# A fifth projection joins the four that are accumulated part by part in the first stage

## The chip, the core and the metric

The kernel runs on one NeuronCore of a Trainium2 chip. Its metric is the device time of one launch in microseconds (us), less being better. Five engines take part: TensorE (PE in the profile, its weight loads PEld), VectorE (DVE), ScalarE (ACT), GpSimd (POOL) and SyncE (SP), which issues nearly all DMA transfers here. Each engine runs its own instructions in a fixed order and waits where an operand or a buffer is not ready.

## The reference

A decoder block on 512 tokens of width 1024. The part that matters here is its beginning:

```python
ada = silu(c) @ w_ada + b_ada                 # 6 vectors of 1024
h = x * (1 + scale1) + shift1
proj = h @ w_in                               # 512 x 2304
qa, ka, va, qb, kb, vb = split(proj)
oa = sliding_window_attention(qa, ka, va)     # 8 heads, 2 key/value heads
ob = stick_breaking_attention(qb, kb, vb)     # 8 heads
mix = concat(rms_norm(oa), rms_norm(ob)) @ w_out
x = layer_norm(alpha * x + gate1 * mix)
```

After it come a second modulation and the PEER layer (product-key retrieval over 16384 experts, computed densely for three of the four token blocks and by gathered rows for the fourth), then the second layer norm.

## The kernel before, in words

All fp32 matrix products are made of three passes. A tile is split into a high part (ACT, a copy to the matmul's type, line 93) and a low part (DVE, the difference, line 94), and high times high, high times low and low times high are accumulated in PSUM. In the profile's names, `hhi` and `hlo` are the two halves of the modulated input, `uhi`/`ulo` and `wpre` those of a projection's weights, `vwhi`/`vwlo` those of the value projection.

**First stage.** The modulation needs `scale1` and `shift1`, and these need 2 x 4 MB of adaLN weights. The work is cut into four parts of 256 columns (PARTS). For each part SP issues the adaLN weights (`wah`, line 212) and the input's columns (`oT`, line 246); PE multiplies the weights by silu(c) (line 221, tile `adap`), ACT copies the result (`rows`, line 224), PE sums it over partitions into four columns (line 227, tile `zada`), DVE adds the bias and makes `sc` (lines 230, 232), and ACT and DVE modulate and split the part's two chunks (lines 266, 268, 93, 94). Four projections are accumulated along with the parts (`half_proj`, line 275): six products of 128 x 512 for each part and projection. They are q and k of the first two pairs of stick-breaking heads. Their weights are loaded by `load_head` (line 251) with parts 0 and 1. What a projection lacks when the last part is modulated is added by `proj_chunk`, which also copies the result out of PSUM (ACT, line 306).

`zada` is a tile of three PSUM banks. The column sums use the first bank, a few warm-up products the second, and the third is free. The same three banks are the score tile `z` of the stick-breaking attention (`sb_weights`): its first product (line 368) waits until `zada` is done with.

**What follows.** In the order of the program text: weights of the first stick-breaking pair (`sb`, high priority), q and k of the second pair, the value projection of the second half of the columns (`proj_v(1)`, line 323, 96 products of 320 columns), `qa` of the first pair of local heads (`proj_chunk(9)`, line 304, 24 products), the gate of the second sub-layer (`ada_rows(5)`: eight multiply-adds on DVE, lines 171 and 173, on weights `wa` loaded at line 167, and a column sum on PE, line 190), the value projection of the first half (`proj_v(0)`), the values of the first pair (`sbv`), the second pair, the other gate (`ada_rows(2)`) and so on. The loads of `wa` and the three tiles of a value projection (`vwraw`, `vwhi`, `vwlo`) share four buffers (tag `big`), so a load waits there until a DVE or PE instruction has freed one.

The order on each engine is set by the Tile framework's scheduler, from the program text and priorities. It mixes these pieces, so that on PE the products of one stand between those of another.

Of the kernel before, what the change touches and what calls it, by code (L numbers as in the profile page):

```python
# [8 lines left out]
F32 = mybir.dt.float32  # L9
F32R = mybir.dt.float32r  # L10
# [10 lines left out]
P = 128  # L21
D = 1024
DC = 8
S = 512
# [21 lines left out]
PARTS = ((0, 2), (2, 4), (4, 6), (6, 8))  # L46
# [8 lines left out]
GROUP = 6  # L55
OWN = 14
PRE = 0

CW = 80
STAIR = [(0, 1, 16, 0), (1, 1, 8, 16), (2, 1, 5, 24), (3, 1, 4, 32),  # L60
# [8 lines left out]
def tile_block(ctx, tc, xr, xT, ccol, wada, bcol, brow, wqk, wv, sinks, gncol, wout,  # L69
               ln1c, ln1r, wq, keys, u_rows, uT, v_rows, ln2r, out):  # L70
    nc = tc.nc
# [20 lines left out]
    def split(src, hi, lo, eng=None):  # L92
        A.activation(hi, src, AF.Copy)  # L93
        (eng or V).tensor_tensor(lo, src, hi.bitcast(F32), op=OP.subtract)  # L94

    def load_split(src, shape, tag, pool, eng=None, rawtag=None, rawbufs=None):
        raw = pool.tile(shape, F32, name=f"{tag}raw", tag=rawtag or f"{tag}raw", bufs=rawbufs)
        nc.sync.dma_start(raw, src)
        hi = pool.tile(shape, F32R, name=f"{tag}hi", tag=f"{tag}hi")
        lo = pool.tile(shape, F32R, name=f"{tag}lo", tag=f"{tag}lo")  # L100
        split(raw, hi, lo, eng)
        return hi, lo
# [40 lines left out]
    with ExitStack() as front:  # L143
# [4 lines left out]
        fw = fw_cm.__enter__()  # L148
        ps = front.enter_context(tc.tile_pool(name="psf", bufs=2, space=PSUM))
# [43 lines left out]
        def load_w_in(i):  # L193
            return load_split(wqk[i].rearrange("p (c n) -> p c n", c=DC), [P, DC, P], "u", wsp)
# [10 lines left out]
        def ada_load(h):  # L205
            c0, c1 = PARTS[h]
            wpart[h] = []
            for q in range(2):
                w = fa.tile([P, 2560], F32, name="wah", tag="big", bufs=BIG)[:, :2048].rearrange(
                    "p (c g n) -> p c g n", c=4, g=2)  # L210
                for g in range(2):
                    nc.sync.dma_start(w[:, :, g], wada[g].rearrange("p (c n) -> p c n", c=DC)[
                        :, 4 * q:4 * q + 4, c0 * P:c1 * P])
                wpart[h].append(w)

        def ada_part(h):
            c0, c1 = PARTS[h]
            p = ps.tile([P, 512], F32, name="adap", tag="o", bufs=1)
            for q, w in enumerate(wpart.pop(h)):
                for j in range(4):  # L220
                    T.matmul(p[32 * j:32 * j + 32, :], srep[:, 4 * q + j], w[:, j].rearrange("p g n -> p (g n)"),
                             start=(q == 0), stop=(q == 1), skip_group_check=True)
            rows = fa.tile([P, D], F32, name="rows", tag="acc")[:, :512]
            A.activation(rows, p, AF.Copy)
            cols = zada[:, 4 * h:4 * h + 4]
            for n in range(4):
                T.matmul(cols[:, n:n + 1], rows[:, n * P:(n + 1) * P], part, start=True, stop=True,
                         skip_group_check=True)
            for g in range(2):
                V.tensor_tensor(adac[:, g * 8 + c0:g * 8 + c1], cols[:, 2 * g:2 * g + 2], bc[:, g * 8 + c0:g * 8 + c1],  # L230
                                op=OP.add)
            V.tensor_scalar(sc1[:, c0:c1], adac[:, 8 + c0:8 + c1], 1.0, None, op0=OP.add)
# [3 lines left out]
        heads = []  # L236
        zada = ps.tile([P, 1536], F32, name="zada", tag="z", bufs=1)

        def warm(n):
            for _ in range(n):  # L240
                T.matmul(zada[:, 512:512 + P], ones, ones, start=True, stop=True, skip_group_check=True)


        def load_x(h):
            for dc in range(*PARTS[h]):
                nc.sync.dma_start(oT[:, dc], xT[:, dc * S:(dc + 1) * S])

        def load_head(i):
            raw = wsp.tile([P, DC, P], F32, name="uraw", tag="uraw") if i < 2 else fw.tile(
                [P, 1536], F32, name="hraw", tag="e", bufs=2)[:, :D].rearrange("p (c n) -> p c n", c=DC)  # L250
            nc.sync.dma_start(raw, wqk[i].rearrange("p (c n) -> p c n", c=DC))
            if i < 2:
                t = [wsp.tile([P, DC, P], F32R, name=f"u{e}", tag=f"u{e}") for e in ("hi", "lo")]
            elif i == 2:
                t = [fw.tile([P, DC, P], F32R, name=f"wpre{e}", tag="prs", bufs=3) for e in range(2)]
            else:
                both = fw.tile([P, 2560], F32R, name="wpre", tag="vr", bufs=1)
                t = [both[:, k * D:(k + 1) * D].rearrange("p (c n) -> p c n", c=DC) for k in range(2)]
            split(raw, *t)
            heads.append((t, ps.tile([P, S], F32, name="pj", tag="mmss"[i], bufs=2)))  # L260

        def modulate(h):
            for dc in range(*PARTS[h]):
                xt = oT[:, dc]
                if dc % 2:
                    A.activation(xt, xt, AF.Identity, scale=sc1[:, dc:dc + 1], bias=adac[:, dc:dc + 1])
                else:
                    V.tensor_scalar(xt, xt, sc1[:, dc:dc + 1], adac[:, dc:dc + 1], op0=OP.mult, op1=OP.add)
                split(xt, hhi[:, dc], hlo[:, dc])

        def half_proj(i, h):
            (hi, lo), p = heads[i]
            for dc in range(*PARTS[h]):
                for n, (a, b) in enumerate(((hi, hhi), (hi, hlo), (lo, hhi))):
                    T.matmul(p, a[:, dc], b[:, dc], start=(dc == 0 and n == 0), stop=(dc == DC - 1 and n == 2))

        warm(WARM[0])
        for h in range(len(PARTS)):
            ada_load(h)
            load_x(h)  # L280
            if h < 2:
                load_head(2 * h)
                load_head(2 * h + 1)
            with tc.high_priority():
                ada_part(h)
                if h == 0:
                    warm(WARM[1])
                modulate(h)
            if h == len(PARTS) - 1:
                break  # L290
            for i in range(min(4, 2 * h + 2)):
                for g in range(h + 1) if i >= 2 * h else (h,):
                    half_proj(i, g)

        def proj_chunk(i, nm):
            if i < 4:
                half_proj(i, len(PARTS) - 1)
                p = heads[i][1]
            else:
                hi, lo = load_w_in(i)  # L300
                p = ps.tile([P, S], F32, name="pj", tag="m", bufs=2)
                for dc in range(DC):
                    for n, (a, b) in enumerate(((hi, hhi), (hi, hlo), (lo, hhi))):
                        T.matmul(p, a[:, dc], b[:, dc], start=(dc == 0 and n == 0), stop=(dc == DC - 1 and n == 2))  # L304
            o = fw.tile([P, S], F32, name=nm, tag=nm)
            A.activation(o, p, AF.Copy, scale=0.125 if nm[0] == "q" else 1.0)
            return o
# [155 lines left out]
        def sb(j, q, k):  # L463
            with tc.high_priority():
                return sb_weights(q, k)

        def sbv(j, w):
            with tc.high_priority():
                sb_values(j, w)

        w = sb(0, proj_chunk(0, "q"), proj_chunk(1, "k"))
        q0, k0 = proj_chunk(2, "q"), proj_chunk(3, "k")
        proj_v(1)
        qa = proj_chunk(9, "qa")
        ada_rows(5, gate2, 1)
        proj_v(0)
        sbv(0, w)
        w = sb(1, q0, k0)
        ada_rows(2, gate1, 0)
        q0, k0 = proj_chunk(4, "q"), proj_chunk(5, "k")  # L480
        sbv(1, w)
        ka = proj_chunk(8, "ka")
        w = sb(2, q0, k0)
# [3 lines left out]
        q0, k0 = proj_chunk(6, "q"), proj_chunk(7, "k")  # L487
# [3 lines left out]
        w = sb(3, q0, k0)  # L491
# [27 lines left out]
        p = ps.tile([P, S], F32, name="ssp", tag="o", bufs=1)  # L519
# [30 lines left out]
        for tb in (1, 2, 3, 0):  # L550
            t = slice(tb * P, (tb + 1) * P)
            zg = [[ps.tile([P, 512], F32, name="zm", tag="ms"[g]) for _ in range(2)] for g in range(2)]
            for n_c, c in enumerate(ORDER):
                hi, lo = wo[c]
# [40 lines left out]
    ps = ctx.enter_context(tc.tile_pool(name="psm", bufs=1, space=PSUM, reuse_waits="tile"))  # L595
# [47 lines left out]
    for hp in range(NHP):  # L643
        hi, lo = load_split(wq[hp].rearrange("p (c n) -> p c n", c=DC), [P, DC, P], "u", wsp, G)
        p = bank("h", "pq", bufs=2)
# [187 lines left out]
    for i in range(groups):  # L833
# [5 lines left out]
        p = banks[i] = bank(f"y{2 + i % 4}", "pw")  # L839
# [156 lines left out]
    plan = [[] for _ in range(NK + 1)]  # L996
    todo = list(range(PRE, 2 * P))
    for n, t in enumerate(todo):
# [52 lines left out]

    for n in range(min(RING, PRE)):
        fetch(n)
    while len(stash) < LOOK:
        u_slot(len(stash), bank("h", "ph", bufs=2), ring.tile([P, ND], F32, name="stash"), V if len(stash) < LOOK - LG else G)
    for n in range(PRE):
        unit(n)
        if n + RING < PRE:
            fetch(n + RING)
# [20 lines left out]
    for i in range(NK):  # L1080
# [6 lines left out]
        p = u_mm(i + LOOK) if i + LOOK < NK else None  # L1087
# [103 lines left out]
```

## Time and profile before

| | us |
|---|---|
| median of 3 runs | 1593.63 |
| lowest and highest | 1587.36, 1598.72 |
| the profiled execution's own time | 1593.33 |
| its span | 1591.6 |
| PE busy | 1552.4 (98%) |
| DVE busy | 1220.5 (77%) |
| ACT busy | 647.0 (41%) |
| POOL busy | 457.4 (29%) |

The profile is of one execution. Its own time differs from the span by 1.7 us of start and end, and from the median by 0.3 us. The attention part that the change touches takes the first 300 us; the PEER layer takes the rest. A matmul's end is modelled and matmuls overlap, so that the distance between starts says how fast they pass, and the duration of one row does not.

### The profile page before, as it was taken

How to read it: one execution, taken by the hardware profiler on the slowest of the kernel's cores; microseconds unless marked ns; L12 is line 12 of the kernel's file. 1: busy time of each engine (PE TensorE's matmuls, PEld its weight loads, DVE VectorE, ACT ScalarE, POOL GpSimd, SP SyncE). 2: the span in 40 equal slices, each digit the busy share in tenths (PEclk: the TensorE clock that was granted, in tenths of full speed). 3: DMA queues.
4: the chain of work that ended last, by engine and by line, in shares of the span. 5: the costliest groups of instructions: out<-in, count | busy, mean ns of one | idle time of the engine just before them, and what ended most of it. 6: DMA issues, size and time to landing. Idle time of an engine off the chain costs nothing.

```text
span 1591.6 us, 21979 instructions
## 1 busy us (share of the span) xinstructions
PE 1552.4 (98%) x8109; PEld 1344.7 (84%) x8109; DVE 1220.5 (77%) x2351; ACT 647.0 (41%) x935; POOL 457.4 (29%) x410
## 2 busy tenths in 40 slices
PE   8999999999989999999999999999999999999997
PEld 5776766788879999899999999999999999998885
DVE  3568485599999997578777777777777777777887
ACT  2535574433354554333333333333333333333340
POOL 0002133544400000334333333333433344333100
PEclk9999899999999999999999999999999999999998
DMA  9563132222225655999999989999898998989872
GB/s 339 198 257 146 53 125 87 92 81 80 93 89 190 225 212 212 328 333 321 310 305 314 316 294 312 310 309 322 295 309 308 314 315 300 313 281 313 269 248 83
DMA packets 147356, 382.12 MB, mean 240 GB/s; under 512 B 11312, under 2 KB 68656, under 8 KB 143280
## 3 DMA queue, kind: packets, MB, share of 16 engines
q1 hardware_dynamic: 110384, 246.49, 44.6%
q0 software_dynamic: 36864, 134.23, 24.6%
q8 instruction: 63, 1.03, 0.3%
q14 instruction: 45, 0.37, 0.1%
HBM read 351.32 MB, written 29.36 MB: 239 GB/s over the span
## 4 chain that ended last, share of the span: by engine, by line
PE 77%; DVE 13%; DMA 4%; ACT 3%; issue 1%; SPq 1%; POOL 1%; DVEq 0%; ACTq 0%; POOLq 0%
PE yb L991 32%; PE ph L981 25%; PE pw L842 5%; PE ph L807 4%; PE pj L304 3%; PE zm L557 2%; DVE scr L621 1%; DMA wa<-in_wada_dram 1%; DVE tsi L623 1%; DVE tsi L620 1%; DMA wah<-in_wada_dram 1%; PE pq L648 1%; DVE tsv L622 1%; DVE tsv L619 1%; PE z L368 1%
## 5 line engine op out<-in xcount | busy, mean ns | idle before, releaser
L856 POOL DMA_INDIRECT gat<-in_u_rows_dram,idx x128 | 162.5, 1269 | 477.6 <-DVE hd L874 226.7
L94 DVE TENSOR_TENSOR ulo<-uraw,uhi 128x1024 fp32r<-128x1024 f32 x133 | 162.7, 1225 | 164.8 <-ACT uhi L93 160.4
L981 PE MATMUL ph<-h2hi,ulo 128*128 128x384 f32 x768 | 258.6, 337 | 0.6 <-DVE ulo L94 0.6
L981 PE MATMUL ph<-h2hi,uhi 128*128 128x384 f32 x768 | 258.2, 336 | 0.6 <-ACT uhi L93 0.6
L981 PE MATMUL ph<-h2lo,uhi 128*128 128x384 f32 x768 | 258.1, 336 | 0.0
L856 POOL DMA_INDIRECT gat<-in_v_rows_dram,idx x128 | 162.1, 1267 | 263.6 <-DVE y L884 227.0
L991 PE MATMUL yb<-vhi,ghi 128*128 128x512 f32 x630 | 195.6, 391 | 0.0
L991 PE MATMUL yb<-vhi,glo 128*128 128x512 f32 x630 | 195.5, 391 | 0.0
L991 PE MATMUL yb<-vlo,ghi 128*128 128x512 f32 x630 | 195.2, 391 | 0.0
L93 ACT ACTIVATE uhi<-uraw 128x1024 fp32r<-128x1024 f32 x155 | 162.3, 1049 | 74.8 <-PE pq L648 52.9
L884 DVE SCALAR_TENSOR_TENSOR y<-gat,cf,y 128x1024 f32<-128x1024 f32 x127 | 162.9, 1283 | 2.8 <-DMA gat<-in_v_rows_dram,idx 0.5
L874 DVE CUSTOM_DVE_ANT_0 gscr<-gat,h2row 128x1024 f32<-128x1024 f32 x128 | 156.5, 1223 | 9.6 <-DMA gat<-in_u_rows_dram,idx 7.2
L1098 ACT ACTIVATE stash<-ph 128x384 f32<-128x384 f32 x96 | 47.2, 492 | 274.9 <-PE ph L981 274.9
L981 PEld LDWEIGHTS ph<-h2hi,uhi 128*128 128x128 f32 x768 | 144.4, 188 | 4.7 <-ACT uhi L93 1.0
L981 PEld LDWEIGHTS ph<-h2lo,uhi 128*128 128x128 f32 x768 | 144.4, 188 | 4.4
L981 PEld LDWEIGHTS ph<-h2hi,ulo 128*128 128x128 f32 x768 | 144.3, 188 | 1.0 <-DVE ulo L94 1.0
L991 PEld LDWEIGHTS yb<-vlo,ghi 128*128 128x128 f32 x630 | 118.2, 188 | 26.3
L991 PEld LDWEIGHTS yb<-vhi,glo 128*128 128x128 f32 x630 | 118.3, 188 | 25.8
L94 DVE TENSOR_TENSOR vlo<-vraw,vhi 128x1024 fp32r<-128x1024 f32 x97 | 118.5, 1222 | 18.9 <-ACT vhi L93 18.3
L991 PEld LDWEIGHTS yb<-vhi,ghi 128*128 128x128 f32 x630 | 117.3, 188 | 17.9
L93 ACT ACTIVATE vhi<-vraw 128x1024 fp32r<-128x1024 f32 x97 | 102.8, 1060 | 56.4 <-issue 39.5
L958 ACT ACTIVATE ghi<-gt 128x384 fp32r<-128x384 f32 x97 | 51.0, 526 | 175.4 <-DVE gt L924 175.4
(311 smaller groups left out, 2898.2 us busy)
## 6 DMA issues: line engine op xcount, KB each, us to landing
uraw<-in_uT_dram SPq DMA_DIRECT2D x128, 512.0 KB
vraw<-in_v_rows_dram SPq DMA_DIRECT2D x128, 512.0 KB
w_d<-stage SPq DMA_DIRECT2D x12, 2048.0 KB
wt<-w_d SPq DMA_DIRECT2D x32, 768.0 KB
wa<-in_wada_dram SPq DMA_DIRECT2D x16, 1024.0 KB
wah<-in_wada_dram SPq DMA_DIRECT2D x16, 512.0 KB
uraw<-in_wq_dram SPq DMA_DIRECT2D x16, 512.0 KB
uraw<-in_wqk_dram SPq DMA_DIRECT2D x11, 512.0 KB
```

Source lines behind the costliest of these rows:

```text
L93: A.activation(hi, src, AF.Copy)
L94: (eng or V).tensor_tensor(lo, src, hi.bitcast(F32), op=OP.subtract)
L304: T.matmul(p, a[:, dc], b[:, dc], start=(dc == 0 and n == 0), stop=(dc == DC - 1 and n == 2))
L807: T.matmul(p[:, :ND], a[:, dc], b[:, dc, P:], start=(dc == 0 and n == 0), stop=(dc == DC - 1 and n == 2))
L842: T.matmul(p[:, k * P:(k + 1) * P], oh4[:, 1, :, k], oh4[:, 2 + j, :, k], start=(j == 0), stop=(j == 1), skip_group_check=True)
L856: G.indirect_dma_start(out=t, out_offset=None, in_=rows, in_offset=bass.IndirectOffsetOnAxis(ap=idx[:, k:k + 1], axis=0))
L874: V.tensor_tensor_reduce(out=scr, in0=t, in1=h2row, scale=1.0, scalar=0.0, op0=OP.mult, op1=OP.add, accum_out=hd[:, n:n + 1])
L884: V.scalar_tensor_tensor(y0, t, cf[:, k:k + 1], y0, op0=OP.mult, op1=OP.add)
L958: A.activation(gop[i][0], gts[i], AF.Copy)
L981: T.matmul(p[:, :ND], a[:, dc], b[:, dc, P:], start=(dc == 0 and n == 0), stop=(dc == DC - 1 and n == 2))
L991: T.matmul(ybank[b][c0 // 512][:, c0 % 512:(c1 - 1) % 512 + 1], x[:, t], y[:, c0:c1], start=(i == 0 and n == 0), stop=(n == 2 and i == (NK ...
L1098: A.activation(stash[i + LOOK], p[:, :ND], AF.Gelu_apprx_tanh)
```

## The change

The table FRONT names the projections of the first stage, now five: 0 to 3 and 9, the queries `qa` of the first pair of local heads. The fifth's weights are loaded and split with part 2, into buffers of tiles that the attention uses later (the raw weights in one of the two `e` buffers, where the raw weights of heads 2 and 3 were, the halves in `sphi` and `splo`). Its result goes into the third bank of `zada`. The products of its first three parts are written behind those of the four, and `proj_chunk(9)` is called ahead of `sb(0, ...)` and no longer behind `proj_v(1)`. Line numbers of the changed kernel are higher by 1 to 8 than those before.

```diff
+FRONT = (0, 1, 2, 3, 9)
...
-            nc.sync.dma_start(raw, wqk[i].rearrange("p (c n) -> p c n", c=DC))
+            nc.sync.dma_start(raw, wqk[FRONT[i]].rearrange("p (c n) -> p c n", c=DC))
...
+            elif i == 4:
+                t = [fw.tile([P, 1536], F32R, name=f"wpre{e}", tag=f"sp{e}", bufs=1)[:, :D].rearrange(
+                    "p (c n) -> p c n", c=DC) for e in ("hi", "lo")]
...
-            heads.append((t, ps.tile([P, S], F32, name="pj", tag="mmss"[i], bufs=2)))
+            heads.append((t, zada[:, 1024:] if i == 4 else ps.tile([P, S], F32, name="pj", tag="mmss"[i], bufs=2)))
...
                 load_head(2 * h + 1)
+            elif h == 2:
+                load_head(4)
             with tc.high_priority():
                 ada_part(h)
...
-            for i in range(min(4, 2 * h + 2)):
+            for i in range(min(len(FRONT), 2 * h + 2)):
                 for g in range(h + 1) if i >= 2 * h else (h,):
                     half_proj(i, g)
 
         def proj_chunk(i, nm):
-            if i < 4:
-                half_proj(i, len(PARTS) - 1)
-                p = heads[i][1]
+            if i in FRONT:
+                n = FRONT.index(i)
+                half_proj(n, len(PARTS) - 1)
+                p = heads[n][1]
...
-        w = sb(0, proj_chunk(0, "q"), proj_chunk(1, "k"))
+        q0, k0 = proj_chunk(0, "q"), proj_chunk(1, "k")
+        qa = proj_chunk(FRONT[4], "qa")
+        w = sb(0, q0, k0)
         q0, k0 = proj_chunk(2, "q"), proj_chunk(3, "k")
         proj_v(1)
-        qa = proj_chunk(9, "qa")
         ada_rows(5, gate2, 1)
```

PE, first stage, from the last part's second adaLN product to the first products on its modulated input. Before (`wpre_200`, `wpre_201` are the halves of the third projection's weights, `wpre` those of the fourth, `part` the constant of the column sum):

```order
L221 MATMUL adap<-wah,srep 32x512 x4
L275 MATMUL pj<-hlo,wpre_200 128x512
L275 MATMUL pj<-hhi,wpre_201 128x512
L275 MATMUL pj<-hhi,wpre_200 128x512
...
L227 MATMUL zada<-part,rows 128x1 x4
L275 MATMUL pj<-hhi,wpre_201 128x512
L275 MATMUL pj<-hlo,wpre 128x512
L275 MATMUL pj<-hhi,wpre 128x512 x2
...
L275 MATMUL pj<-hhi,uhi 128x512 x2
```

And now:

```order
L222 MATMUL adap<-wah,srep 32x512 x4
L279 MATMUL pj<-hhi,wpre 128x512
L279 MATMUL pj<-hlo,wpre 128x512
L279 MATMUL pj<-hhi,wpre 128x512
L279 MATMUL zada<-hhi,wprehi 128x512
L279 MATMUL zada<-hlo,wprehi 128x512
L279 MATMUL zada<-hhi,wprelo 128x512
...
L228 MATMUL zada<-part,rows 128x1 x4
L279 MATMUL pj<-hhi,uhi 128x512 x2
L279 MATMUL zada<-hhi,wprehi 128x512
```

Before, four products stand between the adaLN product and the column sum, and six behind it. Now the six stand ahead of it, 18 products of the fifth projection too, and none between it and the products that need the modulated input.

ACT, from the split of the last part's input (`hhi`) to the first score tile (`e<-z`). Before:

```order
L93 ACTIVATE hhi<-oT 128x512 x2
L306 ACTIVATE q<-pj 128x512
L93 ACTIVATE vwhi<-vwraw 128x2560
L306 ACTIVATE k<-pj 128x512
L306 ACTIVATE q<-pj 128x512
...
L93 ACTIVATE uhi<-uraw 128x1024 x2
L371 ACTIVATE e<-z 128x1280
L372 ACTIVATE e<-e 128x1280
```

And now:

```order
L94 ACTIVATE hhi<-oT 128x512 x2
L94 ACTIVATE vwhi<-vwraw 128x2560
L313 ACTIVATE q<-pj 128x512
L94 ACTIVATE uhi<-uraw 128x1024
L313 ACTIVATE k<-pj 128x512
L313 ACTIVATE qa<-zada 128x512
L94 ACTIVATE uhi<-uraw 128x1024
L378 ACTIVATE e<-z 128x1280
L313 ACTIVATE q<-pj 128x512
L379 ACTIVATE e<-e 128x1280
L313 ACTIVATE k<-pj 128x512
L380 ACTIVATE e<-e 128x1280
```

The split of the value weights now stands ahead of the first q, the copy of `qa` ahead of the scores, and the copies of the second pair's q and k between the steps on the score tile.

PE, from the end of the value projection of the second half to that of the first (both on `vwhi`, `vwlo`). Before:

```order
L323 MATMUL pj<-vwhi,hlo 128x320
L304 MATMUL pj<-hhi,uhi 128x512
L304 MATMUL pj<-hlo,uhi 128x512
L304 MATMUL pj<-hhi,ulo 128x512
...
L383 MATMUL z<-sphi,negtri 128x512 x2
...
L383 MATMUL z<-splo,negtri 128x512 x2
...
L190 MATMUL adap<-acc,ones 128x512 x2
L368 MATMUL z<-q,k 128x512
...
L323 MATMUL pj<-vwhi,hhi 128x320
```

And now:

```order
L330 MATMUL pj<-vwhi,hlo 128x320
L191 MATMUL adap<-acc,ones 128x512 x2
L330 MATMUL pj<-vwhi,hhi 128x320 x2
L390 MATMUL z<-sphi,negtri 128x512 x2
...
L330 MATMUL pj<-vwlo,hhi 128x320
```

The 24 products on `uhi`, `ulo` are gone from here. Two products of the next value projection stand ahead of the `sphi` products; the `splo` products and the next pair's `z<-q,k` now stand inside that projection.

## Rows read from the trace of the kernel before

**Rows 1.** Busy time by engine, the page: time, share of the span, instructions.
```profile
PE 1552.4 (98%) x8109; PEld 1344.7 (84%) x8109; DVE 1220.5 (77%) x2351; ACT 647.0 (41%) x935; POOL 457.4 (29%) x410
```

**Rows 2.** Stretches: engines' busy us (instructions), then PE clock, DMA share, GB/s.
```profile
0.00:40.00 40.00, 32.89 (x168) 22.69 (x168) 12.39 (x31) 11.79 (x17) 2.57 (x11) 0.91 1.00 339
40.00:56.00 16.00, 15.23 (x74) 10.28 (x75) 4.38 (x9) 7.01 (x11) 0.00 (x0) 1.00 0.41 156
```

**Rows 3.** PE in time, last part: start, us, instruction [idle before, releaser].
```profile
41.51 1.06 PE L221 MATMUL adap<-wah,srep 128*32 128x512 f32 x8
...
47.06 0.95 PE L227 MATMUL zada<-part,rows 128*128 128x1 f32 x8
...
49.90 0.73 PE L275 MATMUL pj<-hhi,uhi 128*128 128x512 f32 x2 [0.40 <-ACT hhi L93]
...
55.83 2.42 PE L368 MATMUL z<-q,k 64*128 64x512 f32 x8
```

**Rows 4.** PE in time, 77 to 90 us.
```profile
77.40 0.40 PE L304 MATMUL pj<-hhi,uhi 128*128 128x512 f32 x1
...
82.29 0.40 PE L304 MATMUL pj<-hhi,uhi 128*128 128x512 f32 x1
...
84.39 0.85 PE L383 MATMUL z<-splo,negtri 128*128 128x512 f32 x3
...
85.54 1.93 PE L190 MATMUL adap<-acc,ones 128*128 128x512 f32 x4
87.40 2.42 PE L368 MATMUL z<-q,k 64*128 64x512 f32 x8
89.75 0.42 PE L323 MATMUL pj<-vwhi,hhi 128*128 128x320 f32 x1
```

**Rows 5.** PE in time, the end of the first value sums.
```profile
107.74 0.44 PE L399 MATMUL oacc<-e,vr 128*64 128x128 f32 x4 [0.53 <-ACT vr L325]
108.47 1.98 PE L190 MATMUL adap<-acc,ones 128*128 128x512 f32 x4 [0.29 <-DVE acc L173]
```

**Rows 6.** ACT in time.
```profile
49.23 1.14 ACT L93 ACTIVATE hhi<-oT 128x512 fp32r<-128x512 f32 x2
...
52.79 2.34 ACT L93 ACTIVATE vwhi<-vwraw 128x2560 fp32r<-128x2560 f32 x1
...
56.45 2.02 ACT L93 ACTIVATE uhi<-uraw 128x1024 fp32r<-128x1024 f32 x2
58.34 1.26 ACT L371 ACTIVATE e<-z 128x1280 f32<-128x1280 f32 x1
...
81.05 1.49 ACT L93 ACTIVATE sphi<-e 128x1536 fp32r<-128x1536 f32 x1 [2.40 <-DVE e L378]
```

**Rows 7.** DVE in time.
```profile
27.21 2.36 DVE L94 TENSOR_TENSOR wpre<-hraw,wpre 128x1024 fp32r<-128x1024 f32 x2 [0.18 <-ACT wpre L93]
...
55.16 2.83 DVE L94 TENSOR_TENSOR vwlo<-vwraw,vwhi 128x2560 fp32r<-128x2560 f32 x1 [3.99 <-ACT vwhi L93]
...
62.24 1.49 DVE L375 SCALAR_TENSOR_TENSOR e<-z,e 128x1280 f32<-128x1280 f32 x1
...
65.80 1.28 DVE L173 SCALAR_TENSOR_TENSOR acc<-wa,silu,acc 128x1024 f32<-128x1024 f32 x1
...
84.83 2.82 DVE L94 TENSOR_TENSOR vwlo<-vwraw,vwhi 128x2560 fp32r<-128x2560 f32 x1 [0.50 <-ACT vwhi L93]
```

**Rows 8.** The chain that ended last: start, us, what; an issue to its landing.
```profile
67.11 6.89 DMA wa<-in_wada_dram
...
76.73 5.70 DMA vwraw<-in_wv_dram
```

**Rows 9.** SP's DMA issues in time, adaLN weights of the last part.
```profile
25.75 5.01 SPq L212 DMA_DIRECT2D wah<-in_wada_dram  x4
```

**Rows 10.** Stretches at the lower clock, columns as in rows 2.
```profile
26.20:30.00 3.80, 3.80 (x10) 2.80 (x9) 3.20 (x4) 1.92 (x3) 0.00 (x0) 0.55 1.09 356
183.80:197.40 13.60, 13.60 (x52) 10.15 (x50) 3.56 (x5) 4.05 (x6) 0.99 (x1) 0.51 0.20 68
```

## The prediction, made before the changed kernel ran

> **What bounds the kernel now.** The busy table first: PE is busy 98% of the span [rows 1], so nearly every microsecond taken off PE, or filled where it waits, counts in full. The change touches the first 115 us alone; behind that the order of the engines is the old one but for small swaps inside the attention. So I read PE in order of time there, asking where it waits. While the adaLN weights come in (0 to 40 us) PE is busy 32.9 of 40 us with 339 GB/s moving; from 40 to 56 us it is busy 15.2 of 16 [rows 2]. In the second stretch the fifth projection's products land. There PE waits 0.40 us in one place, for the split of the last part's input [rows 3]. Then PE runs on, and the qa products that are to move stand between 77.40 and 84.4 us [rows 4].
>
> **Their price where they are.** From the first to the 22nd qa product the starts lie 82.29 - 77.40 = 4.89 us apart over 21 steps, 0.233 us each [rows 4]; 24 cost 5.6 us. They cost the same in the first stage. Moving them gains only the PE idle time that they fill, less any that they open. What did they cover? ACT splits the value weights of proj_v(0) when the load issued at 76.73 us has landed 5.70 us later [rows 8], DVE takes the low part until 84.83 + 2.82 = 87.65 us [rows 7], and PE starts on them at 89.75 us [rows 4]. The qa products are that wait's cover, and it goes.
>
> **Part by part.**
>
> *The load.* 512 KB more on SP ahead of the last part's adaLN weights. Its raw buffer is free when DVE has split the third projection's weights, the first of two at 27.21 us, so at 27.21 + 1.18 = 28.4 [rows 7]; SP would have gone on at 25.75 [rows 9] and now does about 0.5 us after 28.4, some 3.1 us later. Queued behind it are those weights, the last input chunks and the value weights. Bytes up to the last adaLN weights: 16 x 0.524 MB of them, 1.57 MB of input, 4 + 1 heads of 0.524 MB, 12.6 MB; at 339 GB/s [rows 2] 37.1 us. PE comes to them at 41.51 us or later [rows 3]. Cost 0, with 4 us of cover; if it were gone, up to 3.1 us.
>
> *The split.* One more split of 128 x 1024 on ACT and DVE, about 1.0 and 1.2 us (half of the pairs in [rows 6] and [rows 7]), behind the third part's modulation, where DVE is busy 4.4 of 16 us [rows 2]. Cost 0; the same split goes further on.
>
> *The last part.* The column sum started at 47.06 us, and the first product on the modulated input at 49.90 [rows 3]. Of these 2.84 us the sums take 0.81 (the chain through DVE and ACT the rest), and six leftover products fill 1.4. In the new order the six and 18 of the fifth stand ahead of the sums and none behind. So the sums start 24 x 0.233 = 5.6 us later, at 52.7, the first product at 55.5, and PE stands 2.0 us in place of about 0.5: **+1.5 us**.
>
> *The scores.* The first score product waits for the copies of k and now of qa, since qa lies in its tile. ACT ends the split of the input at 50.37 + 5.6 = 56.0, then 2.34 for the value weights, and q, a weight split, k and qa at 0.5, 1.0, 0.5, 0.5 (a copy of 128 x 512 takes half of the `hhi` pair's 1.14, a split half of 2.02 [rows 6], less a little overlap): 60.9. PE has 23 products first, 0.237 apart as in the last part now (25 starts from 49.90 to 55.83 [rows 3]): 55.5 + 5.4 = 60.9. A tie; the scores start at 61.0 in place of 55.83 [rows 3], cost 0.1. The attention's chain is thus 5.2 us later, and 6.1 from DVE's step at 62.24 us [rows 7] on, as two copies of 0.5 now stand between ACT's steps.
>
> *The value weights of proj_v(0).* Their load waits for the last multiply-add of ada_rows(5); that for a load issued when the fourth (65.80 us [rows 7]) frees its buffer. In the new order the fourth stands right behind DVE's attention step, which ends at 63.73 + 6.1 = 69.8; it ends at 71.1, 4.0 us later. With 6.89 and 5.70 us from issue to landing as now [rows 8], the low part is ready at 87.65 + 4.0 = 91.6. PE: scores until 63.4, seven products (1.6), proj_v(1) with what is mixed in as before (from 58.2 to 77.40, 19.2 and one product), the gate's sums 1.86 (85.54 to 87.40): ready at 86.3. The high part comes at 88.8, then `sphi` 1.49 behind it on ACT [rows 6] at 90.3. PE waits 2.5 + 1.2 + 0.2: **+3.9**. The old waits of 0.53 and 0.29 us further on [rows 5] should go, as PE is later than what they wait for: **-0.8**.
>
> *Sum:* 1.5 + 0.1 + 3.9 - 0.8 = +4.7 us. By the other route: behind 91.6 PE has what it had from 89.75 to 110.45 us (108.47 + 1.98 [rows 5]) less 0.8 of waits, with 3.5 of `splo` and `z<-q,k` products that stood ahead (1.15 and 2.35 [rows 4]): 91.6 + 23.1 = 114.7 against 110.45, +4.3. I take +4. Bounds of the largest term: if only the value split's delay (58.4 against 55.13, 3.2) reaches it, +3.5 in the sum; if the load keeps its time, the wait is 1.3 and the sum +2; if all 6.1 reach it, +6.5.
>
> **The clock, left out of the sum.** TensorE fell to the lower level, 1.2 GHz, at 26.2 us, after sums over partitions and an idle stretch, for 3.8 us (granted 0.55), and at 183.8 for 13.6 us (0.51), behind column sums of ada_cols [rows 10]. The first costs 3.8 x 0.45 = 1.7 us, the second 13.6 x 0.49 = 6.7. The two new waits resemble the first, 0 to 1.7 each. The new order puts full products between the two column sums at 180 to 190 us: 0 to -6.7. Nothing of before decides these, so 0 in the sum and both ends in the range.
>
> **A rule that speaks against this.** In 40 to 56 us weight loads are busy 10.28 of 16 us [rows 2], yet 25 products start one behind the other from 49.90 to 55.83 us, 0.237 apart [rows 3]. The Trainium skill (Perfetto Trace Analysis, Identifying the Most-Contended Engine) calls matmul busy time a poor measure and has headroom judged by LDWEIGHTS busy share and FLOPs. By it this stretch has 5.7 us to spare and the fifth projection would fit free; the trace's start distances do not agree.
>
> **Rivals.**
> 1. *The room is there* and the products pass in the first stage beside the others. For it: weight loads 64% busy. Against: start distances. Even so the low part of proj_v(0)'s weights comes at 87.65 as now, PE has 23.1 us behind it, and 110.75 stands against 110.45: **1593.6 us**, no change. To gain the 5.6 us, that load would have to move too.
> 2. *Faster:* the low-clock stretch at 183.8 goes. Mechanism: the 14 `sphi` and `splo` products that now stand between the two column sums keep the clock up. Against: ahead of 183.8 small value products and score products on 64 rows had run as well, and these remain. It decides if over 4 of the 6.7 us are saved: 1593.3 + 4.3 - 6.7 = **1591 us**.
> 3. *Clearly slower:* both new waits drop the clock (3.4) and the value weights come at the upper bound (6.5): **1603 us**. It would need two stretches as long as that at 183.8 (13.4) to pass 1609.
> 4. *The load starves the last part* (SP held at 28.4): up to 3.1 more, **1600 us**. Against: 4 us of cover.
>
> **How the numbers follow.** The profiled execution took 1593.33 us, 0.3 under the median, so the sum may be laid on either: 1593.3 + 4 = **1597 us**. Chances: forecast (1595 to 1600) 0.55; rival 1, 0.14; rival 2, 0.16; rivals 3 and 4 up to 1609, 0.12; beyond, 0.03. The range leaves out the outer tails: runs of before lie 6 us below and 5 above their median, so 1589 to 1604. About 1% (16 us) is what a measurement of this kernel can tell from no change: all cases but the last lie within it, so faster 0.02, same 0.94, slower 0.04.
>
> **What would show it.** Right: PE idle about 2 us ahead of the last part's first product (some 55.5 us); scores at 61; proj_v(0)'s low part ready at about 91.6 with PE waiting 3 to 4 us ahead of it; the next projection on `uhi` at 114 to 115 in place of 110.45. Wrong: if the scores start at 56 to 58 (rival 1), if the clock stays up through 180 to 200 (rival 2), if the last part's adaLN product waits for a DMA (rival 4), or if the attention behind 115 us gives the 4 us back from waits that I took to shift with it.

## The result, and the profile after

The changed kernel takes **1601.28 us** (median of 14 runs, 1598.34 to 1606.18) against 1593.55 of the kernel before on the same chip; the ratio is 1.0059, 95% interval 1.0046 to 1.0073. That is 7 to 12 us slower and inside the 1% that I called no change. The forecast was 1597, range 1589 to 1604. The profiled execution took 1603.71 us, its span 1602.0. It lies 2.4 us above the median of its runs, so the two profiles are 10.4 us apart where the medians are 7.7.

The stretches of the changed kernel show where its engines differ (columns as in [rows 2]: busy us of PE, its weight loads, DVE, ACT and POOL, then PE clock, DMA share, GB/s):

```profile
40.00:56.00 16.00, 13.62 (x68) 9.35 (x69) 3.84 (x8) 4.26 (x7) 0.00 (x0) 1.00 0.51 195
77.00:90.00 13.00, 10.80 (x57) 8.31 (x55) 6.52 (x8) 7.29 (x7) 2.45 (x4) 1.00 0.40 142
90.00:115.00 25.00, 23.39 (x128) 19.28 (x129) 14.28 (x10) 4.65 (x6) 2.24 (x2) 0.93 0.66 231
184.00:198.00 14.00, 14.00 (x89) 10.89 (x88) 7.21 (x8) 5.43 (x8) 0.77 (x2) 0.87 0.35 114
258.00:276.00 18.00, 11.91 (x31) 7.96 (x29) 12.26 (x23) 7.45 (x11) 4.72 (x2) 0.72 0.66 234
```

Two of these stretches in the kernel before:

```profile
90.00:115.00 25.00, 24.15 (x136) 19.14 (x136) 14.01 (x13) 6.38 (x9) 0.51 (x1) 1.00 0.82 307
258.00:276.00 18.00, 17.00 (x76) 13.57 (x75) 13.34 (x26) 6.89 (x12) 10.01 (x4) 0.98 0.45 154
```

Three things stand there. PE stands longer than before at 40 to 56 and 77 to 115 us, as forecast. At 184 to 198 us its clock is 0.87, where [rows 10] show 0.51; the low stretch is not gone, it comes some 10 us later and lasts about half as long, with 0.81, 0.50 and 0.84 in the three stretches of 4 us from 192 to 204:

```profile
196.00:200.00 4.00, 4.00 (x18) 3.07 (x17) 0.00 (x0) 1.18 (x3) 0.00 (x0) 0.50 0.20 78
```

And at 258 to 276 us, far behind the change, PE is busy 11.91 us in place of 17.00, at a clock of 0.72. The last I had not looked at: it is the largest.

The starts of the same work in the profiled executions tell where each microsecond came and went. The three right columns are experiments, below.

| start of, us | before | changed | after_oldmap | before_newmap | after_lng_behind |
|---|---|---|---|---|---|
| first product of the last part | 49.90 | 55.64 | 55.45 | 51.75 | 55.87 |
| projection behind proj_v(0) | 110.38 | 117.28 | 115.48 | 111.99 | 116.22 |
| values of the third pair | 197.62 | 201.48 | 196.42 | 199.39 | 197.15 |
| column sums `ssp` | 251.2 | 255.6 | 250.6 | 253.2 | 251.4 |
| first transposes `zt` | 264.6 | 276.4 | 264.2 | 273.0 | 265.6 |
| first `pq` | 310.7 | 324.0 | 310.2 | 319.1 | 313.7 |
| last `yb<-vhi,ghi` | 1513.9 | 1528.2 | 1513.3 | 1522.7 | 1516.5 |
| span | 1591.6 | 1602.0 | 1588.4 | 1597.9 | 1592.1 |

Read the column of the changed kernel against before: +5.7, +6.9, then +3.9 and +4.4 (some 3 us come back), then +11.8 and +13.3 within 60 us, and +14.3 to the end of the long stage. The last stretch, 73.8 us in place of 77.7, gives 3.9 back.

**The first part.** PE of the changed kernel in time, around the last part (answers to [rows 3]):

```profile
52.80 0.95 PE L228 MATMUL zada<-part,rows 128*128 128x1 f32 x8
55.64 0.73 PE L279 MATMUL pj<-hhi,uhi 128*128 128x512 f32 x2 [1.89 <-ACT hhi L94]
...
61.19 1.98 PE L375 MATMUL z<-q,k 64*128 64x512 f32 x5
```

The sums start at 52.80 (forecast 52.7), the first product at 55.64 (55.5) after 1.89 us of waiting (2.0), the scores at 61.19 (61.0). Then PE around proj_v(0) of the changed kernel:

```profile
90.77 0.56 PE L330 MATMUL pj<-vwhi,hhi 128*128 128x320 f32 x2 [2.97 <-ACT vwhi L94]
92.15 1.43 PE L390 MATMUL z<-sphi,negtri 128*128 128x512 f32 x3 [0.81 <-ACT sphi L94]
```

and DVE, whose multiply-adds free the buffer for that load and which makes the low part:

```profile
73.58 1.28 DVE L174 SCALAR_TENSOR_TENSOR acc<-wa,silu,acc 128x1024 f32<-128x1024 f32 x1 [1.73 <-DMA wa<-in_wada_dram]
...
90.75 2.82 DVE L95 TENSOR_TENSOR vwlo<-vwraw,vwhi 128x2560 fp32r<-128x2560 f32 x1 [1.62 <-ACT vwhi L94]
```

The load was issued at 80.40 us and landed 8.0 us later, not 5.70 as in [rows 8], so the low part is ready at 93.57 (forecast 91.6). PE waits 2.97 + 0.81 us and 1.06 for `splo` at 76.6. The `negtri` products at 92.15 also run at the lower clock (0.57 granted from 92 to 96 us): three in 1.43 us, where three took 0.85 at 84.39 us before [rows 4].

**The second loss.** SP issues its transfers in order. Its DMA issues behind the attention, changed kernel:

```profile
257.63 0.33 SPq L545 DMA_DIRECT2D lng<-in_ln1r_dram  x1
258.06 0.38 SPq L547 DMA_DIRECT2D lnb<-in_ln1r_dram  x1
258.49 0.42 SPq L549 DMA_DIRECT2D l1c<-in_ln1c_dram  x1
258.96 1.50 SPq L568 DMA_DIRECT2D r<-in_xr_dram  x3
```

and before:

```profile
229.65 0.33 SPq L537 DMA_DIRECT2D lng<-in_ln1r_dram  x1
231.44 0.33 SPq L539 DMA_DIRECT2D lnb<-in_ln1r_dram  x1
231.82 0.42 SPq L541 DMA_DIRECT2D l1c<-in_ln1c_dram  x1
232.30 2.40 SPq L560 DMA_DIRECT2D r<-in_xr_dram  x3
```

The same transfers stand some 27 us later. SP's longest wait between 225 and 262 us in the changed kernel (what waited for what, us in total, times, longest):

```profile
SPq L545 <- PE ssp L530: 23.8, 1, 23.8
```

The layer norm's scale `lng` now waits for the column sums `ssp`, which have nothing to do with it. Behind it on SP wait `r`, the block's input rows. The chain of waits of the changed kernel goes through just that (start, us, what):

```profile
258.96 6.37 DMA r<-in_xr_dram
265.33 0.02 issue
265.35 1.06 ACT r L569
266.42 0.03 issue
266.44 0.81 DVE r L573 x2
```

In the kernel before, that DVE step starts at 257.77. The reason is not in any order of instructions. The change gives the tags `sphi` and `splo` their first tiles in the fifth load, earlier than before, and the pool lays tags out in order of first use. Addresses of the two built programs, in bytes of a partition:

```
                        lies over, before      lies over, changed
lng  113888 to 117984   k, sphi                neg, sqa
lnb  117984 to 122080   sphi, splo             sqa, sink, dist, q
sqa's own place         102016 to 106112       114304 to 118400
```

`sqa` is what the `ssp` sums read, so it is free only when they end.

### The profile page after: what moved, and what is told of

It is laid out like the page before. It is cut to its first block, busy times and chain, and to the rows that moved or that the text cites. A ratio compares the mean times of both kernels' runs of the same rounds, so it can differ in the third digit from the quotient of the medians.

```text
span 1602.0 us, 21970 instructions
## 1 busy us (share of the span) xinstructions
PE 1553.3 (97%) x8109; PEld 1345.2 (84%) x8109; DVE 1224.7 (76%) x2351; ACT 647.9 (40%) x935; POOL 457.1 (29%) x410
## 4 chain that ended last, share of the span: by engine, by line
PE 81%; DVE 11%; DMA 3%; ACT 2%; issue 1%; POOL 0%; SPq 0%; DVEq 0%; ACTq 0%; POOLq 0%
PE yb L999 33%; PE ph L989 25%; PE pw L850 5%; PE ph L815 4%; PE pj L311 3%; PE zm L565 2%; DVE scr L629 1%; PE pj L279 1%; DVE tsi L631 1%; DVE tsi L628 1%; PE pj L330 1%; PE z L375 1%; PE pq L656 1%; DVE tsv L630 1%; DVE ulo L95 1%
```

## The experiments

All ratios are to the kernel before on the same chip, with 95% intervals; times are medians. The runs were taken on several chips, so that ratios, not times, are compared between them. In the cuts of code, `...` stands for lines left out.

### The memory map, both ways

**before_newmap**: the kernel before with only the tiles' first use moved.

```
+            elif h == 2:
+                for e in ("hi", "lo"):
+                    fw.tile([P, 1536], F32R, name=f"held{e}", tag=f"sp{e}", bufs=1)
```

> The kernel before with one thing of the change alone: the memory map. Two tiles with the tags sphi and splo are allocated (and never used) where the change first allocates them, so that the tiles allocated later move up and lng, loaded behind the attention, comes to lie over sqa. No engine's order of instructions changes. Theory M (map): the load of lng, and the loads of lnb, l1c and the first r behind it on SP, wait for the column sums of sqa (251.25 us in the kernel before) and are issued at about 253 to 256 in place of 229.65; the r chain on DVE is late and the first transposes zt start at 272 to 273 in place of 264.63; time +7.4 to +9 us, 1601 to 1603, about as much as the whole change. Theory S (shift): the loss at 258 to 276 us comes from the attention being later, the map does nothing: 1593.6, zt at 264.6.

Measured: 1601.51 us, ratio **1.0052** (1.0036 to 1.0069). SP waits for the same sums:

```profile
SPq L540 <- PE ssp L525: 23.8, 1, 23.8
```

`lng` is issued at 255.22 us, `zt` starts at 273.0, and PE at 258 to 276 us looks as in the changed kernel:

```profile
258.00:276.00 18.00, 12.74 (x44) 9.43 (x44) 12.05 (x24) 6.47 (x9) 7.49 (x4) 0.82 0.64 244
```

Two unused tiles cost as much as the whole change. (Of the +8.4 at `zt`, 2.0 stand at `ssp` already: this profiled execution had PE at 0.83 over the first 40 us, not 0.91.)

**after_oldmap**: the changed kernel with the old layout.

```
             elif h == 2:
+                for nm, n, bufs in (("negtri", P, 1), ("negone", P, 1), ("neg", P, 1), ("sqa", 2 * S, 1),
+                                    ("sink", NH, 1), ("dist", 2 * P, 1), ("q", S, 2), ("k", S, 2)):
+                    fw.tile([P, n], F32, name=f"held{nm}", tag=nm, bufs=bufs)
                 load_head(4)
```

> The changed kernel with the memory map of the kernel before: ahead of the fifth load the tags negtri, negone, neg, sqa, sink, dist, q and k are allocated once in the old order (unused tiles), so lng lies over sphi again. No engine's order of instructions changes. Theory M: lng's load is issued 3 to 5 us later than the 229.65 us of before, not at 257.6; the wait of DVE's r at 267 and the low clock at 260 to 280 go; time 7.4 to 9 us below the changed kernel's 1601.3: 1592.3 to 1594, so that the change by itself costs nearly nothing. Theory S: 1601.3 as the changed kernel.

Measured: 1593.45 us, ratio **1.0006** (0.9988 to 1.0024). `lng` is issued at 230.44, `zt` starts at 264.2. Theory S falls, theory M stands in both directions: the map carries the loss, and the moved projection by itself costs 0.9 us, not separable from nothing. Its stretches:

```profile
90.00:115.00 25.00, 24.71 (x135) 19.90 (x135) 13.41 (x11) 3.03 (x6) 1.91 (x2) 0.93 0.66 234
184.00:198.00 14.00, 14.00 (x92) 9.98 (x93) 7.46 (x8) 5.69 (x8) 2.04 (x3) 1.00 0.31 108
...
258.00:276.00 18.00, 17.00 (x77) 13.57 (x76) 12.79 (x26) 6.77 (x12) 9.99 (x4) 0.99 0.39 139
```

Here the early loss of 5.1 us (115.48 against 110.38) is there and gone again at 197 us (-1.2): the clock at 184 to 198 us is 1.00, and 13.6 us at 0.51 are worth 6.7. (This execution took 1590.10 us, 3.4 less than the median of its runs, so the starts show more of that gain than a usual run has.)

**after_lng_behind**: the changed kernel, new map, with the transfers that are needed first ahead of `lng` and `lnb` on SP.

```
-        nc.sync.dma_start(lng, ln1r[0:1, :].to_broadcast([P, D]))
...
-        nc.sync.dma_start(lnb, ln1r[1:2, :].to_broadcast([P, D]))
...
+        for tb in (1, 2, 3):
+            early[tb] = fo.tile([P, D], F32, name="r", bufs=3)
+            behind = nc.sync.dma_start(early[tb], xr[tb * P:(tb + 1) * P, :])
+        with tc.issue_after(behind.ins):
+            nc.sync.dma_start(lng, ln1r[0:1, :].to_broadcast([P, D]))
+            nc.sync.dma_start(lnb, ln1r[1:2, :].to_broadcast([P, D]))
...
```

> The changed kernel with its own memory map (lng over sqa), but the loads of l1c and of the first three r tiles stand ahead of those of lng and lnb on SP. If the map costs time only since loads that are needed wait on SP's queue behind lng: the r loads are issued 3 to 5 us after the 229.7 to 234.7 us of the kernel before, DVE's r step is on time, first zt at about 269 in place of 276.38, and the time is 7 us lower than the changed kernel's: ratio to the kernel before 1.000 to 1.002. Rival: lng itself is needed as early, or what stands behind lng on SP (weights of the next stage) is, and the loss stays or moves to 276 to 310 us: ratio 1.005 to 1.006.

Measured: 1593.8 us, ratio **1.0010** (0.9998 to 1.0022). SP's issues here:

```profile
229.63 0.38 SPq L547 DMA_DIRECT2D l1c<-in_ln1c_dram  x1
230.05 6.04 SPq L559 DMA_DIRECT2D r<-in_xr_dram  x3
253.37 0.33 SPq L561 DMA_DIRECT2D lng<-in_ln1r_dram  x1
```

`lng` still waits for the sums, until 253.37, and nobody minds: `zt` starts at 265.6, earlier than the 269 I expected. So the loss is the queue behind `lng`, not `lng`. A mended order on SP and a mended map are worth about the same, 8 us. (Behind the sums this edit also moves a few instructions on the other engines; ahead of them PE's order is that of the changed kernel.)

### The places that the prediction priced

**after_sums_first**: the fifth's 18 products are held until the last part's column sums are issued.

```
+                with tc.issue_after(sums.ins):
+                    for g in range(h):
+                        half_proj(4, g)
...
-            for i in range(min(len(FRONT), 2 * h + 2)):
+            for i in range(min(4, 2 * h + 2)):
```

> The changed kernel with the last part's column sums ahead of the 18 products of the fifth projection instead of behind them. If the +1.5 us that I put on the last part is a matter of that order: sums at 48.6 us in place of 52.80, the wait of 1.89 us ahead of the last part's first product goes, that product starts at 53.7 in place of 55.64, the scores at about 59.3, and the time is 1.9 us lower, 1599.4. Rival: the gain is taken back at the scores or ahead of proj_v(0)'s low part, which wait for ACT and DMA: 1601.3.

Measured: 1597.17 us, ratio 1.0038 (1.0024 to 1.0053), against 1.0059 (1.0046 to 1.0073) of the changed kernel: some 3 us less, but the intervals overlap. The wait is gone; 0.32 us of another remain:

```profile
50.07 1.04 PE L228 MATMUL zada<-part,rows 128*128 128x1 f32 x8
51.43 0.50 PE L280 MATMUL zada<-hhi,wprehi 128*128 128x512 f32 x1 [0.32 <-DVE adac L231]
...
55.73 0.40 PE L280 MATMUL pj<-hhi,uhi 128*128 128x512 f32 x1
```

The last part's product starts no earlier in this execution, as its first 40 us ran at 0.83 and the part came 1.5 us later; in after_map_ka_sums below, with 0.91, it starts at 53.84 (53.7 was expected). So that order did cost the last part's start its 1.5 us; what of it reaches the kernel's time this run does not settle. (The new wait I had not seen: the sums lie in the same tile, `zada`, as the fifth's result.)

**after_ka_cover**: `ka = proj_chunk(8, "ka")` is traced behind `proj_v(1)`, where `qa` was, not behind `sbv(1, w)`.

> The changed kernel with the projection of ka traced where that of qa stood before, behind proj_v(1), instead of behind the second pair's values. Theory C (cover): the 4.8 us that PE waits between 76 and 93 us for splo, vwhi and sphi are there since the 24 qa products (5.6 us) no longer stand ahead; 24 ka products fill them again: time 4 to 5 us lower, 1596.5 to 1597.3. Rival: the waits go but the place the ka products leave at 120 to 150 us opens as much: 1600 to 1602; or ka's load pushes the adaLN weights back on SP and the waits stay: 1601 to 1604.

Measured: 1599.27 us, ratio 1.0058 (1.0036 to 1.0079): the time does not tell it from the changed kernel. The two waits of 2.97 and 0.81 us came down to one of 0.2, and the low clock went with them:

```profile
77.00:90.00 13.00, 13.00 (x69) 11.13 (x70) 6.52 (x7) 8.53 (x8) 2.51 (x4) 1.00 0.41 146
90.00:115.00 25.00, 24.93 (x138) 19.51 (x138) 16.35 (x13) 4.96 (x7) 1.21 (x2) 1.00 0.62 216
```

So it is the missing products that opened the wait at proj_v(0), and that wait is what the clock fell in. What it is worth in time stays open: in the profiled executions `ssp` starts 4.6 us earlier than in the changed kernel, the medians, of two sets of runs, are 2 us apart, the ratios not at all.

**before_filled**: the kernel before with 16 products whose result is not used. In the program they stand behind the first of the two groups of column sums; on PE seven follow that group and nine come ahead of the second.

```
+            if g == 3:
+                for n in range(16):
+                    T.matmul(p[:, P:], hhi[:, 0, :P], hhi[:, 1, P:], start=True, stop=True, skip_group_check=True)
```

> The kernel before with 16 extra products on the whole array (128 x 384 of the modulated input, into unused columns of the first ada_cols result; their result is not used) around the two groups of column sums at 180 to 192 us, where TensorE is granted 0.53 from 184 to 198 us. Some places on the other engines swap with it. Theory Q: the changed kernel gets its early loss back there since full products stand between the column sums and the score products on 64 rows; then the granted clock of 184 to 198 us is above 0.9 here too, which gives 6.7 us back, and the 16 products cost 16 x 0.175 = 2.8: time 3.9 us lower, ratio 0.9975. Rival: the low level comes whatever stands there: granted 0.5 to 0.6 and 2.8 us slower, ratio 1.0018.

Measured: 1588.37 us, ratio **0.9977** (0.9962 to 0.9991): faster, with more work. The score products in the kernel before, then PE in this run:

```profile
182.74 3.84 PE L368 MATMUL z<-q,k 64*128 64x512 f32 x8
```

```profile
180.98 1.84 PE L180 MATMUL adap<-ones,acc 128*128 128x1 f32 x16
182.68 1.47 PE L184 MATMUL adap<-hhi 128*128 128x384 f32 x7
...
184.67 2.42 PE L371 MATMUL z<-q,k 64*128 64x512 f32 x8
```

```profile
184.00:200.00 16.00, 16.00 (x100) 11.73 (x100) 6.30 (x8) 8.73 (x12) 2.42 (x2) 1.00 0.27 96
```

The score products that took 3.84 us at the low level take 2.42. Theory Q holds for this place: with full products between the column sums and the products on 64 rows the clock stays up, and the third pair's values start at 192.91 us in place of 197.62 (3.9 us earlier was expected). In the changed kernel it is 14 `sphi` and `splo` products, and a few small ones, that stand between the two groups of sums. There the clock is 1.00 from 184 to 192 us and falls behind the second group (184.66 and 190.88 are the two groups' starts), at the score products on 64 rows. after_oldmap and after_lng_behind have that order too and stay at 1.00 to 204 us, so the order alone does not settle it; that the 14 products do it was not tried. The profile shows PE busy all through [rows 10]. The Trainium skill (TensorE: Matmul & The Clock Gate, What's actually happening) puts the low level down to an idle PE; by that rule a stretch with PE busy 13.60 of 13.60 us would not be low. Read off the profile's busy time, the trace does not agree.

### Putting it together

**after_map_ka**: the old map and `ka` in the place of `qa`.

> The changed kernel with the old memory map and with ka projected where qa was. If the two effects are independent: the map takes 8 us off the changed kernel, ka 2 to 4.4: ratio to the kernel before 1.0006 - (0.0013 to 0.0028) = 0.9978 to 0.9993, 1588 to 1591. Rival: with the map mended the attention's end is bound by DVE and POOL, and ka gives nothing: 1.0006.

Measured: 1592.02 us, ratio 1.0000 (0.9986 to 1.0014). Less than the sum of the two. At proj_v(0) it gains what after_ka_cover gained, and at 184 us it loses, the clock being lower than the 1.00 of after_oldmap:

```profile
184.00:200.00 16.00, 15.74 (x83) 12.42 (x84) 10.29 (x16) 5.99 (x7) 1.54 (x4) 0.83 0.19 66
```

**after_map_ka_sums**: after_map_ka with the sums first as well.

> As after_map_ka, and the last part's column sums ahead of the fifth's 18 products. If all three add up: a further 1.6 us off, ratio 0.9968 to 0.9983, 1586 to 1590. Rival: the 1.6 us are taken back at proj_v(0) or in the attention: same as after_map_ka.

Measured: 1588.93 us, ratio **0.9980** (0.9966 to 0.9994): as expected, and faster than both kernels, by some 3 us against before. The low clock has moved to where the two groups of sums now stand one behind the other:

```profile
176.00:180.00 4.00, 3.74 (x23) 3.65 (x22) 0.17 (x1) 2.58 (x8) 0.00 (x0) 0.64 0.00 0
180.00:184.00 4.00, 3.74 (x11) 3.10 (x12) 2.23 (x6) 0.03 (x1) 0.77 (x2) 0.51 0.01 2
```

**after_combined_apart**: to part them, `qa2 = proj_chunk(11, "qa")` was traced ahead of `ada_cols(4)` and that held behind nine of its products.

```
...
-        ada_cols(4)
+        qa2 = proj_chunk(11, "qa")
+        with tc.issue_after(at[11][8]):
+            ada_cols(4)
...
-        qa2 = proj_chunk(11, "qa")
```

> after_map_ka_sums with the column sums of ada_cols(4) set behind nine products of the next projection instead of directly behind those of ada_cols(3). In after_map_ka_sums the granted clock is 0.64 and 0.51 from 176 to 184 us behind the two groups of sums; if the two groups one behind the other do that, it is 1.00 here and the time about 3.4 us lower: ratio to the kernel before 0.996. Rival: the clock falls after the second group alone, later: 0.998 as after_map_ka_sums.

Measured: 1595.31 us, ratio 1.0025 (1.0013 to 1.0037). A miss, on both theories. The two groups now start at 177.16 and 194.49 us, and the clock falls behind each of them: 0.90 and 0.68 from 176 to 184 us, 0.57 from 196 to 200. So it is not only the one group directly behind the other that does it. And a later stretch, where after_map_ka_sums stays at 1.00, is now at the low level:

```profile
236.00:240.00 4.00, 4.00 (x12) 2.85 (x12) 1.56 (x8) 1.57 (x7) 0.00 (x0) 0.50 0.23 80
240.00:244.00 4.00, 2.02 (x7) 1.64 (x7) 2.67 (x9) 1.89 (x4) 0.53 (x2) 0.50 0.29 114
```

That it is the products moved up that are missing there is likely, but was not tested.

**after_combined_filled**: after_map_ka_sums with six products that do nothing behind each group of sums.

> after_map_ka_sums with six extra products of 128 x 384 (result not used) behind each of the two groups of column sums of ada_cols, which stand one behind the other at 175 to 181 us there. As in before_filled, the granted clock behind them should stay at 1.00 in place of 0.64 and 0.51 from 176 to 184 us: 7.4 us at 0.57 cost about 3.2 us, the 12 products 2.1: 1.1 us lower, ratio to the kernel before 0.997. Rival: the clock stays low and the products cost 2.1 to 4: 0.9995 to 1.0005.

Measured: 1589.98 us, ratio 0.9987 (0.9971 to 1.0003). The time, between the two expectations, tells little. About the clock the rival is right: with the two groups of sums and only six products between them it is low all the same:

```profile
180.00:184.00 4.00, 4.00 (x22) 4.00 (x23) 1.52 (x8) 1.74 (x2) 0.00 (x0) 0.68 0.00 0
184.00:188.00 4.00, 4.00 (x15) 3.42 (x14) 3.52 (x4) 1.54 (x2) 0.00 (x0) 0.50 0.30 90
```

What before_filled showed holds for its place. How much work of which kind is enough, these runs do not say.

## Why the prediction came out, and where it was wrong

The time lies in the range, and the sign of the sum was right. The sum was not: +4 was forecast, and what came is the early loss, a gain that I had left out, and a loss that I had not seen. So it is in part luck that the range holds: its upper end was set for other reasons, and no rival has the loss that brought the time near it. The time lies outside the 1595 to 1600 that had 0.55, where rivals 3 and 4 stood with 0.12, and neither is what happened.

- **Load and split, 0:** right. No adaLN product of the last part waits for a DMA; rival 4 did not come.
- **Last part, +1.5:** right, 1.89 us of waiting in place of 0.40 [rows 3], and after_sums_first took it out.
- **Scores, +0.1:** right, 61.19 for 61.0.
- **Value weights of proj_v(0), +3.9:** right in kind, too small. The two waits that I priced came to 2.97 + 0.81 = 3.78 us (2.5 + 1.2 forecast), but not as worked out: PE was ready for the weights at 87.80 us, not at 86.3, in part as it had waited 1.06 us for `splo`, which I had not forecast, and the load took 8.0 us to land, not 5.70. On top of the priced waits come those 1.06 us and about 1.7 of the lower clock (0.93 over 25 us, which I had kept out of the sum with 0 to 1.7). after_oldmap runs the same orders on every engine, and there the load landed in 5.6, the low part came at 91.52 (forecast 91.6) and the projection behind started +5.1, not +6.9. One profiled execution gives such a landing only roughly. (The other route's +4.3 has a slip: 20.7 less 0.8 and with 3.5 is 23.4, not 23.1, so +4.6.)
- **Old waits, -0.8:** they are gone.
- **Rival 1, the room is there:** no. The fifth's 18 products stand 0.233 us apart and took their 4.2 us, as the start distances had it and the share of weight loads had not. The other measure that the prediction's rule names, FLOPs, I did not work out.
- **"The clock, left out of the sum", with rival 2 at 0.16:** wrong as a term of 0. The low stretch at 183.8 us came later and half as long in the changed kernel and not at all in the profiled after_oldmap, and gave 3 to 6.7 us back. The price stood in [rows 10] and the mechanism in my text. before_filled shows that full products in this place can keep the clock up; that the `sphi` and `splo` products did it is not shown.
- **The shift, taken as rigid behind 115 us:** the step that failed. It rested on "behind that the order of the engines is the old one but for small swaps". From the column sums `ssp` on it holds on every engine without a single swap, and between the old and the new map the orders do not differ in one instruction; the waits do. I read what the fifth's split does to `sphi` and `splo` as buffers, and not that a tag's first use sets the addresses of all that is laid out after it. The price is 8.3 us (ratio 1.0052): with it and the clock's 3 to 6.7 us back the sum would have been +6 to +9.

By the parts: +6.9 at 115 us, 3.0 back by 197, +7.4 from `ssp` to `zt`, +2.5 to the end of the long stage, and 3.9 back in the last 77 us. The last two are not explained: with before as the measure, all the profiled executions here have a shorter end, so it may be the one of before that is long.

## What to carry to other kernels

When a change gives a buffer its first use at another place, compare the addresses of the two builds, not the orders alone: ask of each later load what it now lies over, when that is free, and what stands behind the load on its queue. Put transfers that are needed first ahead of those that may wait. And a stretch at the lower clock next to the moved work is a term of the sum, with a sign, not a tail of the range.

## What the runs showed of the hardware that was not expected

Of the 7.4 us from `ssp` to `zt` about half is not spent on waiting for the late transfer itself, but on what the late steps then met. DVE of the changed kernel, the layer norm's small steps:

```profile
270.64 0.15 DVE L107 TENSOR_SCALAR l1tm<-l1mv 128x1 f32<-128x1 f32 x1
...
271.30 1.47 DVE L112 TENSOR_TENSOR l1tm<-l1rs 128x1 f32<-128x1 f32 x1 [0.50 <-ACT l1rs L109]
272.80 2.30 DVE L113 TENSOR_TENSOR l1tm<-l1tm 128x1 f32<-128x1 f32 x1
275.13 0.15 DVE L114 TENSOR_SCALAR l1tm<-l1tm 128x1 f32<-128x1 f32 x1
```

and POOL in the same stretch:

```profile
270.37 4.72 POOL L95 TENSOR_TENSOR ulo<-uraw,uhi 128x1024 fp32r<-128x1024 f32 x2 [14.80 <-ACT uhi L94]
```

Before, the two DVE steps `TENSOR_TENSOR` took 0.16 us each and fell between two of POOL's operations. Now the first ends at 272.77 and the second at 275.10, where POOL's two end (272.73 and 275.09): a step on 128 numbers waited for an operation of 2.36 us to end, twice, 3.4 us on the way to `zt`. before_newmap shows it too (1.43 and 2.27). The Trainium skill (SBUF — State Buffer, Who interferes with whom) says that a DVE instruction with two inputs in SBUF and a GpSimd instruction that reads SBUF exclude each other; the trace agrees: the one-input step at 270.64 us ran inside POOL's first operation and took 0.15.
